# The first RMS norm's reciprocal square roots by one power on GpSimd for each half of the rows

## The chip, the cores and the metric

The kernel runs on one core of a Trainium2 chip. The core has TensorE (matrix products and transposes), VectorE, ScalarE and GpSimd for elementwise work, and SyncE, whose queue issues nearly all transfers. The metric is the time of one execution on the device in microseconds, the median of several runs; less is better.

## The reference

The program computes one layer of a hybrid decoder for 1024 rows of 1024 numbers. It begins with an RMS norm:

```python
def rms_norm(x, g):
    xf = x.astype(jnp.float32)
    y = xf * lax.rsqrt(jnp.mean(xf * xf, axis=-1, keepdims=True) + EPS)
    return (y * g.astype(jnp.float32)).astype(x.dtype)
...
    h = rms_norm(x, norm_mix_g)
    proj = h @ w_in
```

The columns of `proj` feed a gated delta rule, an attention over keys that an indexer selects, and two gates. Their merged result goes through an output product onto `x`; a second norm and a squared-ReLU MLP follow. The change is in the first norm alone: in the 1024 values of `rsqrt(mean + EPS)`, one for each row.

## The kernel before

The 1024 rows are eight blocks of 128, one row to a partition, in two halves of four blocks. `norm1(half)` (L279) prepares a half: ScalarE sums the squares of three blocks and VectorE those of the fourth, which gives `nss`, four columns for a half; VectorE makes `nms`, the mean plus EPS; ten small operations of `rsq_w` (L103) make `nr`, its reciprocal root, from a bit-level first guess and three Newton steps. The blocks are then scaled by `nr` (the first half in the tiles `pj`, by VectorE; the second in tiles that a profile calls `w` and `irl`, shared by VectorE and ScalarE). TensorE transposes them into the PSUM banks `sq`, two groups of 128 columns at a time, and there are two such banks. `ht_out` (L322) takes each group out twice: ScalarE writes `hh`, the rounded value times the norm's gain, and VectorE writes `hl`, what the rounding left over. A bank is free for the next transposes when `hl` has been taken from it.

Around this stand other works of the same microseconds. `turn_raw` transposes the first half's blocks without the norm and multiplies them with the first weights (`sc`, `ikh` and `iq` in a profile), so that TensorE has products before `nr` is known. `weights` splits the weight tiles `wraw` and `iq` into a rounded part (ScalarE) and a rest (VectorE). `dense` multiplies `hh` and `hl` with these parts; it sets most of TensorE's work until the attention begins.

No engine chooses its next instruction on the chip. The works are generators that a planner (`Weave`) interleaves while the program is recorded, by estimated times and priorities; `_Ordered` records every operation (all of them therefore carry L2502), and each engine then runs its own list in that order, waiting on semaphores where an operand is not ready. A later part of the kernel already takes such roots in one GpSimd instruction: `roots` (L1693) for the second norm's `nr` and two places in the delta rule (`rk`, `fo`). They raise to the power in `mhalf` (L127), a column of −0.5 behind the tile `vecs`, by whose name a profile shows it.

Of the kernel before, what the change touches and what calls it, by code (L numbers as in the profile page):

```python
# [15 lines left out]
OP = mybir.AluOpType  # L16
# [4 lines left out]
P = 128  # L21
# [29 lines left out]
def body(tc, a, out, dbg=None):  # L51
# [4 lines left out]
    def pool(name, bufs=1, side=None, space=None):  # L56
        kw = {}
        if space is not None:
            kw["space"] = space
        elif side is not None:  # L60
            kw["side"] = side
        if space is not DRAM:
            kw["reuse_waits"] = "tile"
        es = ExitStack()
        p = es.enter_context(tc.tile_pool(name=name, bufs=bufs, **kw))
        return p, es
# [16 lines left out]
    cst, cst_es = pool("cst", side="left")  # L83
# [16 lines left out]
    V_, A_, G_, PE_, SY_ = (wv.engine(e, n) for e, n in ((V, "V"), (A, "A"), (G, "G"), (PE, "PE"), (SY, "SY")))  # L100


    def rsq_w(pl, dst, src, n, tag, apart=True):  # L103
        t = pl.tile([P, max(n, 4)], F32, name=tag + "t")[:, :n]
        V_.tensor_scalar(dst.bitcast(I32), src.bitcast(I32), -0.5, float(0x5F3759DF), op0=OP.mult, op1=OP.add)
        for _ in range(3):
            if apart:
                yield
            V_.scalar_tensor_tensor(t, dst, -0.5, src, op0=OP.mult, op1=OP.mult)
            if apart:  # L110
                yield
            V_.tensor_tensor(t, t, dst, op=OP.mult)
            if apart:
                yield
            V_.scalar_tensor_tensor(dst, t, 1.5, dst, op0=OP.add, op1=OP.mult)
# [11 lines left out]
    mhalf = vecs[:, NV:]  # L127
# [4 lines left out]
    nss, nms, nr = (cst.tile([P, NB], F32, name=n) for n in ("nss", "nms", "nr"))  # L132
# [146 lines left out]
    def norm1(half):  # L279
        bs = slice(half * 4, half * 4 + 4)  # L280
        for tb in (4, 6, 7, 5) if half else range(4):
            yield ("x", tb)
            if tb == 4:
                yield ("x", 7)
                yield ("w1hi",)
                yield ("hhi", 0, 3)
            if tb in (3, 5):
                junk = ix.tile([P, S], F32, name="ikl")
                V_.tensor_tensor_reduce(out=junk, in0=xs[tb], in1=xs[tb], op0=OP.mult, op1=OP.add, scale=1.0,
                                        scalar=0.0, accum_out=nss[:, tb:tb + 1])  # L290
                continue
            junk = scp.tile([P, S], BF16, name="tkeq")
            A_.activation(junk, xs[tb], AF.Square, accum_out=nss[:, tb:tb + 1])
        yield
        if half:
            yield ("norm", 0)
        V_.tensor_scalar(nms[:, bs], nss[:, bs], 1.0 / D, EPS, op0=OP.mult, op1=OP.add)
        yield from rsq_w(cst, nr[:, bs], nms[:, bs], 4, "n2", apart=False)
        yield
        yield 1.2  # L300
        wv.done("norm", half)
        for c in range(2):
            for tb in range(4 * half, 4 * half + 4):
                xc = xs[tb][:, c * HALF:(c + 1) * HALF]
                if tb % 2 and half:
                    A_.activation(xc, xc, AF.Copy, scale=nr[:, tb:tb + 1])
                else:
                    V_.tensor_scalar(xc, xc, nr[:, tb:tb + 1], None, op0=OP.mult)
            if c == 0:
                t = wv.t  # L310
        wv.t = t
        yield
        for k in range(0, KT, 2):
            if k > 2 or half:
                yield ("ht", half - (k < 4), (k - 3) % KT)
            ps = ps_.tile([P, 2, HALF], F32, name="sq")
            for j in range(2):
                for i in range(4):
                    PE_.transpose(ps[:, j, i * P:(i + 1) * P], xs[4 * half + i][:, (k + j) * P:(k + j + 1) * P], ident)
                wv.add(0, ht_out(half, k + j, ps[:, j, :]))  # L320

    def ht_out(half, k, ps):  # L322
        g = gm[:, k:k + 1]
        if half:
            yield 0.2
        A_.activation(ht_hi[k][half], ps, AF.Copy, scale=g)
        wv.done("hhi", half, k)
        yield
        V_.scalar_tensor_tensor(ht_lo[k][half], ps, g, ht_hi[k][half].bitcast(F32), op0=OP.mult, op1=OP.subtract)
        yield  # L330
        wv.done("ht", half, k)
# [532 lines left out]
    for half in range(2):  # L864
        wv.add(half, norm1(half))
# [1708 lines left out]
```

## Time and profile before

| | us |
|---|---|
| median of 3 runs | 1741.82 |
| lowest and highest run | 1741.39, 1743.05 |
| the profiled execution | 1743.84 |
| its span, first to last instruction | 1742.1 |
| TensorE busy in the span | 1730.6 |
| VectorE, ScalarE, GpSimd busy | 1271.5, 1038.3, 590.1 |
| GpSimd busy from 10 to 50 us | 0.0 |

All times below are counted from the start of the span. The granted clock of TensorE was 0.999 of full speed over the run. A row of a timeline gives start, length, engine, line, operation, the tile written and the tiles read; rows of the same form that follow each other are merged (x4), and brackets tell how long the engine had been idle and what it waited for. In the chain of waits each piece is time that could not be shorter without the piece before it.

### The profile page before, as it was taken

The numbers are of one execution on the slowest core, as the hardware profiler recorded it, in microseconds if no ns is written. First come the engines' busy times: TensorE is split into PE (matmuls) and PEld (weight loads), VectorE is DVE, ScalarE is ACT, GpSimd is POOL, SyncE is SP. The second block draws the span as 40 slices with busy tenths as digits, with TensorE's granted clock in tenths as the row PEclk, the third lists the DMA queues.
The fourth block names the chain that finished last, engine by engine and source line by source line (L and its number), as shares of the span: only waits on it lengthen the run. The fifth ranks groups of instructions, "written<-read, shape, count | busy, mean of one in ns | idle before, by whom it ended". The sixth has DMA issues, their size and how long they took to land.

```text
span 1742.1 us, 27140 instructions
## 1 busy us (share of the span) xinstructions
PE 1730.6 (99%) x9451; PEld 1454.7 (84%) x9451; DVE 1271.5 (73%) x2300; ACT 1038.3 (60%) x2304; POOL 590.1 (34%) x793
## 2 busy tenths in 40 slices
PE   9999999999999999999999999999999999999999
PEld 7987998888888888888888888888888888888887
DVE  6668568767888897896477686768666677958673
ACT  7466647766777656555366676757776754333331
POOL 0005531654563553655014121413322323522230
PEclk9999999999999999999999999999999999999999
DMA  5631246646786778755475222335445459473241
GB/s 169 156 75 61 74 133 135 155 123 135 161 204 137 173 161 188 165 132 127 137 244 159 70 81 73 110 111 204 139 142 164 160 216 332 133 241 117 97 145 49
DMA packets 441643, 252.14 MB, mean 145 GB/s; under 512 B 234089, under 2 KB 385826, under 8 KB 441506
## 3 DMA queue, kind: packets, MB, share of 16 engines
q1 hardware_dynamic: 441490, 250.41, 51.0%
q8 instruction: 74, 1.21, 0.3%
q14 instruction: 63, 0.52, 0.1%
q10 hardware_dynamic: 16, 0.00, 0.0%
HBM read 169.97 MB, written 80.38 MB: 144 GB/s over the span
## 4 chain that ended last, share of the span: by engine, by line
PE 94%; ACT 2%; DMA 1%; DVE 1%; issue 1%; POOL 1%; SPq 1%; POOLq 0%; DVEq 0%; ACTq 0%
PE dd L2502 57%; PE o L2502 16%; PE s L2502 7%; PE pt L2502 6%; PE cc L2502 2%; PE sq L2502 2%; PE tt L2502 2%; PE oo L2502 2%; PE jj L2502 1%; DMA w<-in_x_dram 1%; SPq L2502 1%; DMA kd<-TDk 0%; POOL hl L2502 0%; ACT pr L2502 0%; ACT hh L2502 0%
## 5 line engine op out<-in xcount | busy, mean ns | idle before, releaser
L2502 PE MATMUL dd<-hh,w 128*128 128x512 f32 x1552 | 510.1, 401 | 0.0
L2502 PEld LDWEIGHTS dd<-hh,w 128*128 128x128 f32 x1552 | 286.8, 189 | 51.6
L2502 PE MATMUL dd<-hl,w 128*128 128x512 f32 x776 | 310.3, 400 | 0.0
L2502 ACT ACTIVATE m<-m 128x512 f32<-128x512 f32 (+1 forms) x240 | 140.0, 625 | 74.0 <-PE dd L2502 27.7
L2502 DVE TENSOR_TENSOR m<-m,m 128x512 fp32r<-128x512 f32 (+2 forms) x184 | 141.1, 795 | 42.9 <-ACT m L2502 37.5
L2502 PEld LDWEIGHTS dd<-hl,w 128*128 128x128 f32 x776 | 146.3, 189 | 25.5
L2502 PE MATMUL dd<-hh,m 128*128 128x512 f32 x504 | 167.0, 395 | 0.2 <-DVE w L2502 0.2
L2502 PE MATMUL dd<-w,hh 128*128 128x256 f32 (+1 forms) x704 | 165.3, 325 | 0.0
L2502 PEld LDWEIGHTS dd<-w,hh 128*128 128x128 f32 x704 | 118.1, 191 | 9.4 <-issue 0.2
L2502 POOL TENSOR_TENSOR sx<-sx,stmp 128x60 f32<-128x60 f32 (+24 forms) x248 | 114.2, 461 | 19.4
L2502 PE MATMUL dd<-w,hl 128*128 128x256 f32 (+1 forms) x352 | 114.1, 324 | 0.0
L2502 PEld LDWEIGHTS dd<-hh,m 128*128 128x128 f32 x504 | 93.9, 188 | 18.3 <-issue 0.6
L2502 POOL TENSOR_TENSOR stmp<-sx,um 128x60 f32<-128x60 f32 (+24 forms) x186 | 82.1, 442 | 79.5 <-DMA QT<-ot 21.7
L2502 DVE TENSOR_SCALAR_CACHE_REDUCE tkeq<-sc,cand 128x384 f16<-128x384 f32 (+3 forms) x128 | 103.0, 805 | 1.9 <-POOL sc L2502 0.6
L2502 DVE TENSOR_TENSOR w<-w,w 128x1024 fp32r<-128x1024 f32 (+1 forms) x63 | 72.3, 1147 | 43.7 <-ACT w L2502 29.9
L2502 POOL TENSOR_TENSOR m<-m,m 128x512 f32<-128x512 f32 x48 | 67.0, 1405 | 102.5 <-ACT m L2502 54.8
L2502 ACT ACTIVATE hh<-m 128x1024 fp32r<-128x1024 f32 x44 | 44.9, 1055 | 94.4 <-PE s L2502 40.7
L2502 PE MATMUL dd<-hl,m 128*128 128x512 f32 x252 | 99.4, 395 | 0.0
L2502 ACT ACTIVATE ha<-m 128x1024 fp32r<-128x1024 f32 x44 | 45.2, 1056 | 83.3 <-PE s L2502 30.8
L2502 PE MATMUL o<-hh,m 128*128 128x512 f32 x264 | 84.9, 390 | 0.0
L2502 ACT ACTIVATE tkcm<-sc,cand 128x1024 f16<-128x1024 f32 x64 | 73.0, 1141 | 1.0 <-POOL sc L2502 0.6
L2502 PEld LDWEIGHTS dd<-w,hl 128*128 128x128 f32 x352 | 67.2, 191 | 4.8 <-DVE hl L2502 0.2
(424 smaller groups left out, 4357.5 us busy)
## 6 DMA issues: line engine op xcount, KB each, us to landing
HD<-m SPq DMA_DIRECT2D x112, 256.0 KB, 2.3
m<-HD SPq DMA_DIRECT2D x56, 512.0 KB, 3.9
w<-in_w_in_dram SPq DMA_DIRECT2D x48, 512.0 KB, 4.4
m<-in_w_mlp_up_dram SPq DMA_DIRECT2D x33, 512.0 KB, 5.4
m<-in_w_mlp_down_dram SPq DMA_DIRECT2D x16, 512.0 KB, 5.2
w<-in_x_dram SPq DMA_DIRECT2D x10, 512.0 KB, 4.2
wraw<-in_w_in_dram SPq DMA_DIRECT2D x4, 1024.0 KB
es<-GC SPq DMA_DIRECT2D x8, 512.0 KB, 4.5
```

The costliest lines, as they stand in the source:

```text
L2502: ins = f(*args, **kw)
```

## The change

One line of `norm1` changes. The ten VectorE operations on 128 x 4 numbers become one GpSimd operation on 128 x 4 numbers, for each half:

```diff
         if half:
             yield ("norm", 0)
         V_.tensor_scalar(nms[:, bs], nss[:, bs], 1.0 / D, EPS, op0=OP.mult, op1=OP.add)
-        yield from rsq_w(cst, nr[:, bs], nms[:, bs], 4, "n2", apart=False)
+        G_.tensor_tensor(nr[:, bs], nms[:, bs], mhalf.to_broadcast([P, 4]), op=OP.pow)
         yield
         yield 1.2
         wv.done("norm", half)
```

`rsq_w` stays for one later use. Because the planner makes the order, the built programs show what moved. VectorE, at the second half of the rows, with what each instruction waits for (`w_230` is block 4; `hl_107` to `hl_111` are still rows of the first half; before, then now):

```order
L2502 TENSOR_SCALAR nms<-nss 128x4 [waits DVE_49,Activation_49]
L2502 TENSOR_SCALAR nr<-nms 128x4 [waits DVE_49]
L2502 SCALAR_TENSOR_TENSOR n2t<-nr,nms 128x4 [waits DVE_49]
L2502 TENSOR_TENSOR n2t<-n2t,nr 128x4 [waits DVE_49]
L2502 SCALAR_TENSOR_TENSOR nr<-n2t,nr 128x4 [waits DVE_49]
...
L2502 SCALAR_TENSOR_TENSOR hl_107<-sq,gm,hh_106 128x512 [waits PE_49,Activation_49]
L2502 SCALAR_TENSOR_TENSOR hl_109<-sq,gm,hh_108 128x512
L2502 SCALAR_TENSOR_TENSOR hl_111<-sq,gm,hh_110 128x512 [waits PE_49,Activation_49]
L2502 TENSOR_SCALAR w_230<-w_230,nr 128x512 [waits DMAHW0_49,DVE_49]
```

```order
L2502 TENSOR_SCALAR nms<-nss 128x4 [waits DVE_49,Activation_49]
L2502 SCALAR_TENSOR_TENSOR hl_107<-sq,gm,hh_106 128x512 [waits PE_49,Activation_49]
L2502 SCALAR_TENSOR_TENSOR hl_109<-sq,gm,hh_108 128x512
L2502 SCALAR_TENSOR_TENSOR hl_111<-sq,gm,hh_110 128x512 [waits PE_49,Activation_49]
L2502 TENSOR_SCALAR w_230<-w_230,nr 128x512 [waits DMAHW0_49,Pool_49]
```

The ten operations are gone (of the last three of them, which come three times, one set is shown); `hl` now stands right behind `nms`, and the scaling of block 4 waits for GpSimd. In the first half, likewise, the scaling of `pj` stands right behind `nms` and waits for GpSimd. On GpSimd itself the two powers are inserted behind the memsets of the program's start and ahead of the masks of the indexer's scores:

```order
 L2502 MEMSET iq 128x8x40
 L2502 MEMSET sc_150 128x128
+L2502 TENSOR_TENSOR nr<-nms,vecs 128x4 x2
 L2502 AFFINE_SELECT sc_146<-sc_146 128x128
 L2502 AFFINE_SELECT sc_147<-sc_147 128x128
```

Nothing else moved: but for these rows and the numbers of later buffers, the lists of TensorE, VectorE, ScalarE, GpSimd and SyncE are the same, and on ScalarE only the first scaling of the second half waits for GpSimd in place of VectorE.

## The prediction

> **What bounds the kernel now.** I read the page's engine summary first, then its chain that ended last, then the windows of the first 50 us, since the edited code runs only there, then the chain and the timeline of those microseconds row by row.
>
> ```profile
> span 1742.1 us, 27140 instructions
> PE 1730.6 (99%) x9451; PEld 1454.7 (84%) x9451; DVE 1271.5 (73%) x2300; ACT 1038.3 (60%) x2304; POOL 590.1 (34%) x793
> ...
> PE 94%; ACT 2%; DMA 1%; DVE 1%; issue 1%; POOL 1%; SPq 1%; POOLq 0%; DVEq 0%; ACTq 0%
> ```
>
> TensorE is busy for 99% of the span and carries 94% of the chain: the whole run holds 1742.1 − 1730.6 = 11.5 us in which TensorE does nothing. A change away from TensorE can win only what it takes out of these. The windows tell how many of them lie near the first norm (columns: length, then busy time of PE, PEld, DVE, ACT and POOL, then the granted clock and the DMA share):
>
> ```profile
> 10.00:20.00 10.00, 9.17 (x43) 5.57 (x42) 8.34 (x24) 8.10 (x13) 0.00 (x0) 1.00 0.95 338
> 20.00:30.00 10.00, 8.82 (x64) 7.43 (x62) 8.97 (x24) 9.94 (x18) 0.00 (x0) 1.00 0.50 152
> 30.00:40.00 10.00, 9.33 (x63) 8.30 (x62) 8.62 (x17) 5.96 (x10) 0.00 (x0) 1.00 0.01 2
> 40.00:50.00 10.00, 10.00 (x82) 9.82 (x81) 5.39 (x10) 4.44 (x7) 0.00 (x0) 1.00 0.36 117
> ```
>
> TensorE idles 0.83, 1.18 and 0.67 us in the first three, 2.7 us together, and not at all from 40 us. GpSimd is empty from 10 to 50 us, so nothing is queued ahead of the new powers. Between 20 and 30 us it is ScalarE that has no gap (9.94 of 10.00), and the chain there runs through it:
>
> ```profile
> 25.30 1.31 ACT hh L2502 x3
> ...
> 27.00 0.75 ACT w L2502
> ...
> 27.77 0.74 DVE hl L2502
> ...
> 30.10 0.67 DVE hl L2502
> ...
> 30.91 1.06 PE sq L2502 x8
> ```
>
> None of the twenty instructions that go stands in this chain; VectorE enters it at 27.77, after the last of them.
>
> **The change, first half of the rows.** The timeline of VectorE, ScalarE and TensorE around it (start, length, instruction, idle time before):
>
> ```profile
> 10.94 0.17 DVE L2502 TENSOR_SCALAR nms<-nss 128x4 f32<-128x4 f32 x1
> 11.15 0.17 DVE L2502 TENSOR_SCALAR nr<-nms 128x4 int32<-128x4 int32 x1
> ...
> 13.12 3.26 DVE L2502 TENSOR_SCALAR pj<-pj,nr 128x512 f32<-128x512 f32 x8
> 13.15 4.46 PE L2502 MATMUL dd<-sc,iq 128*128 128x512 f32 x10
> ...
> 17.45 1.91 PE L2502 MATMUL sq<-ident,pj 128*128 128x128 f32 x16
> ...
> 18.52 2.42 ACT L2502 ACTIVATE hh<-sq,gm 128x512 fp32r<-128x512 f32 x4 [1.79 <-PE sq L2502]
> ...
> 19.82 0.75 DVE L2502 SCALAR_TENSOR_TENSOR hl<-sq,gm,hh 128x512 fp32r<-128x512 f32 x1 [1.17 <-ACT hh L2502]
> ```
>
> Removed: ten operations from 11.15 to 13.12, 1.97 us of VectorE. Added: one power of 4 elements per partition. The trace has it with 1, 2 and 8 elements, on the same constant operand (of rk and fo: shortest, median and longest in ns, first and last start; of nr: sum in us, mean in ns):
>
> ```profile
> L2502 POOL TENSOR_TENSOR rk<-ke,vecs x8: 1633/1644/1654, 286.2 to 741.7; 128x8 f32<-128x8 f32 x8
> ...
> L2502 POOL TENSOR_TENSOR nr<-nms,vecs 128x2 f32<-128x2 f32 x3 | 2.1, 710 | 1.8 <-DVE nms L2502 1.8
> L2502 POOL TENSOR_TENSOR nr<-nms,vecs 128x1 f32<-128x1 f32 x2 | 1.1, 560 | 0.1
> ...
> 962.59 0.17 DVE L2502 TENSOR_SCALAR nms<-nss 128x2 f32<-128x2 f32 x1
> ...
> 962.83 0.71 POOL L2502 TENSOR_TENSOR nr<-nms,vecs 128x2 f32<-128x2 f32 x1 [0.24 <-DVE nms L2502]
> ...
> L2502 POOL TENSOR_TENSOR fo<-fe,vecs x8: 1633/2064/3065, 407.7 to 864.7; 128x8 f32<-128x8 f32 x8
> ```
>
> From 2 to 8 elements it grows by (1644 − 710) / 6 = 156 ns each, so four cost 710 + 2 × 156 = 1.02 us. The way there is 962.83 − 962.76 = 0.07 us; the way back I set equal, 0.07. From the end of nms to the first user of nr that is 1.16 us against 13.12 − 11.11 = 2.01, so VectorE scales pj 0.85 us earlier, at 12.27. Bounds of the power: from below the 0.71 of two elements; from above the 3.07 that eight took at worst while VectorE was at work (fo's longest). I take 1.02, since VectorE is idle while it waits here.
>
> What is it worth? TensorE works through the raw products (sc, iq) from 13.15 until the transposes of pj at 17.45, and the four tiles that these read first were scaled by 13.12 + half of 3.26 = 14.75: 2.7 us to spare already. VectorE then falls idle for 1.17 us anyway, until ScalarE's hh, which waited 1.79 us for TensorE's sq. The 0.85 us joins that idle time: **0.0 us**. The cover is 1.17 us, so a path through GpSimd of up to 2.01 + 1.17 = 3.18 us costs nothing either.
>
> **The change, second half of the rows.** Here something moves:
>
> ```profile
> 24.38 0.17 DVE L2502 TENSOR_SCALAR nms<-nss 128x4 f32<-128x4 f32 x1 [0.68 <-ACT tkeq L2502]
> 24.58 0.17 DVE L2502 TENSOR_SCALAR nr<-nms 128x4 int32<-128x4 int32 x1
> 24.73 1.26 ACT L2502 ACTIVATE hh<-sq,gm 128x512 fp32r<-128x512 f32 x2
> 24.73 2.42 ACT L2502 ACTIVATE hh<-sq,gm 128x512 fp32r<-128x512 f32 x4
> ...
> 26.36 0.17 DVE L2502 SCALAR_TENSOR_TENSOR nr<-n2t,nr 128x4 f32<-128x4 f32 x1
> 26.45 2.07 DVE L2502 SCALAR_TENSOR_TENSOR hl<-sq,gm,hh 128x512 fp32r<-128x512 f32 x3
> ...
> 27.00 0.74 ACT L2502 ACTIVATE w<-w,nr 128x512 f32<-128x512 f32 x1
> ...
> 29.46 1.06 ACT L2502 ACTIVATE w<-iq 128x1024 fp32r<-128x1024 f32 x1
> 30.41 1.27 ACT L2502 ACTIVATE hh<-sq,gm 128x512 fp32r<-128x512 f32 x2
> 30.91 0.41 PE L2502 MATMUL sq<-ident,w 128*128 128x128 f32 x2 [0.67 <-DVE hl L2502]
> ...
> 31.71 1.41 DVE L2502 SCALAR_TENSOR_TENSOR hl<-sq,gm,hh 128x512 fp32r<-128x512 f32 x2 [0.95 <-ACT hh L2502]
> 33.36 0.38 PE L2502 MATMUL sq<-ident,w 128*128 128x128 f32 x2
> ```
>
> The power runs from 24.62 to 25.64. VectorE no longer waits for nr before hl; it is free at 24.55. But hl needs hh, and these rows show hl starting when the second hh of a pair ends (30.41 + 1.27 = 31.68, hl at 31.71). Of the four hh from 24.73 to 27.15 the first two end at 25.99, so hl starts at 26.03 in place of 26.45: of 1.90 us freed, **0.42** is used. VectorE keeps this 0.42 through the three hl, the four scalings and the fourth hl, whose end at 30.01 + 0.75 = 30.76 lets TensorE start the next transposes 0.15 later. That start moves from 30.91 to 30.49.
>
> ScalarE gains nothing: its w<-w,nr at 27.00 follows hh without a gap and had its nr, done at 26.53, waiting. Now nr is there at 25.71, with 1.29 us to spare in place of 0.47. So w, the rounding of iq at 29.46 and hh at 30.41 stay where they are, and with them the pair of hl at 31.71, which ends at 33.12. The next transposes need the bank that this pair reads: earliest 33.12 + 0.15 = 33.27. TensorE, 0.42 early, would come at 32.94 and wait; before it came at 33.36. Left of the 0.42: 33.36 − 33.27 = **0.1 us**. From 40 us TensorE has no gap, so I let the 0.1 stand to the end.
>
> **Sum.** 0.0 + 0.1 = 0.1 us less. The profiled execution took 1743.84 us, 1.7 around its span of 1742.1 and 2.0 above the runs' median of 1741.82; against the median I say **1741.7 us**, no change. This kernel's measurement can tell about 0.2% (3.5 us) from no change. The ends of the power's price: at 0.71 the sum stays, as nr is nowhere last; at 3.07 the first half still costs nothing (0.07 + 3.07 + 0.07 = 3.21, against the 3.18 of cover), and in the second nr comes at 27.76, holds ScalarE's w by 0.76 and the pair of hl with it, so that the transposes come at 34.03: 0.7 us more.
>
> **Rivals.** (1) *The ten operations are on the path.* Then both halves' gains count: 0.85 + 1.90 = 2.75 us, 1739.1. For it speaks TensorE's wait of 0.67 us for hl at 30.91; against it that ScalarE is full from 20 to 30 us and that the chain of waits has no n2t. A part of it, that the 0.42 survives whole because the pair of hl at 31.71 is not what holds the bank, gives 1741.4.
>
> (2) *GpSimd starts its first arithmetic late, and the kernel becomes slower.* Before, its first two-operand operation comes at 131.97; now it would be the power at 11 us, with the DMA at 95% in the window. The price decides from 3.18 us in the first half and, in the second, from 1.16 + 1.29 = 2.45 us of path. The rows give little for it:
>
> ```profile
> 131.97 5.05 POOL L2502 TENSOR_TENSOR pj<-pj,qng 128x2048 f32<-128x2048 f32 x1 [2.37 <-DVE pj L2502]
> 169.77 4.60 POOL L2502 TENSOR_TENSOR pj<-pj,qng 128x2048 f32<-128x2048 f32 x1 [7.05 <-DVE cand L2502]
> ```
>
> The first is 0.45 us longer than its twin. Once 0.45 on 1.16 is inside the cover. If every path took 4 us, the second half would cost 4.0 − 2.45 − 0.1 = 1.5 us, 1743.3 (the first half's excess of 0.8 us ends ahead of the same gate and isn't added); to be over 3.5 us slower it needs a path of 6.1 us. The rows side against that: 0.45 us, and the earliest of the eight rk, at 286.2 the program's first power, lies with the rest between 1633 and 1654 ns. The Trainium skill speaks for it (GPSIMD Engine Reference, Instruction dispatch): the first call of a freshly loaded kernel on that engine pays about 6 us, which no instruction shows. By an estimate from that page the first path would be 1.16 + 6 = 7.2 us, hl near 19.8 would come 4.0 us late, and the time would be at most 1745.8.
>
> (3) *The shift changes when transfers of later stages meet.* A tenth of a microsecond has no such lever in the rows, but one of either sign of a few us can't be excluded.
>
> **How the numbers follow.** The forecast with its neighbours from −0.4 to +0.7 us: 0.85. Rival 1 whole: 0.05, still inside 0.2%. Rival 2: 0.05, a fifth of it past 3.5 us. Rival 3: 0.05, evenly either side. Faster by over 0.2% is half of rival 3 and a quarter of rival 1, should more follow from it: 0.04. Slower is the other half of rival 3 and the far fifth of rival 2: 0.04. The rest, 0.92, is no change. The range goes nearly down to rival 1 at 1739.1 and takes in the runs' own scatter (1741.39 to 1743.05) and rival 2 at a path of 4 us: 1739.4 to 1743.9.
>
> **What would show it.** In the changed profile: two powers of about 1.02 us near 11.2 and 24.6; pj scaled from 12.3; VectorE idle longer before hl near 19.8; hl at 26.0; ScalarE's rows from 24.7 to 31.7 unmoved; TensorE's transposes at 30.5 and then at 33.3, with an idle entry before these that was not there. It would be wrong if ScalarE's w<-w,nr waited for GpSimd, if hl after 31 us moved with the rest, or if the spans differ by more than 3 us.

## The result, and the profile after

| | before | after |
|---|---|---|
| median, us | 1742.28 | 1760.42 |
| lowest and highest run | 1741.39, 1743.05 | 1759.26, 1760.56 |
| the profiled execution | 1743.84 | 1760.52 |
| its span | 1742.1 | 1758.8 |

Before has one run more here than in the table ahead of the prediction. The ratio is 1.0101 with a 95% interval of [1.0088, 1.0113]: the kernel became about 18 us slower, where 1741.7 was forecast with a range of 1739.4 to 1743.9. The prediction was wrong, by 16.7 us between the two profiled spans.

The page of the kernel after, its span and its engines:

```profile
span 1758.8 us, 27122 instructions
PE 1747.3 (99%) x9451; PEld 1452.6 (83%) x9451; DVE 1273.0 (72%) x2280; ACT 1038.8 (59%) x2304; POOL 592.3 (34%) x795
```

TensorE is idle for 1758.8 − 1747.3 = 11.5 us, exactly as before. All of the 16.7 us is therefore TensorE *busy* time (1730.6 to 1747.3), with the same 9451 products. No engine waits longer anywhere that counts; the products themselves take longer.

Before following that, the stretch that the prediction spoke of. The timeline of the kernel after, first half of the rows and then second half (start, length, instruction, idle time before):

```profile
10.87 0.17 DVE L2502 TENSOR_SCALAR nms<-nss 128x4 f32<-128x4 f32 x1
11.13 1.02 POOL L2502 TENSOR_TENSOR nr<-nms,vecs 128x4 f32<-128x4 f32 x1 [8.85 <-DVE nms L2502]
...
12.19 3.26 DVE L2502 TENSOR_SCALAR pj<-pj,nr 128x512 f32<-128x512 f32 x8 [1.14 <-POOL nr L2502]
...
15.92 2.36 DVE L2502 TENSOR_TENSOR w<-wraw,w 128x1024 fp32r<-128x1024 f32 x2 [0.48 <-ACT w L2502]
...
19.64 0.75 DVE L2502 SCALAR_TENSOR_TENSOR hl<-sq,gm,hh 128x512 fp32r<-128x512 f32 x1 [1.35 <-ACT hh L2502]
...
24.19 0.17 DVE L2502 TENSOR_SCALAR nms<-nss 128x4 f32<-128x4 f32 x1 [0.68 <-ACT tkeq L2502]
24.44 1.02 POOL L2502 TENSOR_TENSOR nr<-nms,vecs 128x4 f32<-128x4 f32 x1 [12.29 <-DVE nms L2502]
...
25.83 2.07 DVE L2502 SCALAR_TENSOR_TENSOR hl<-sq,gm,hh 128x512 fp32r<-128x512 f32 x3 [1.47 <-ACT hh L2502]
...
26.82 0.74 ACT L2502 ACTIVATE w<-w,nr 128x512 f32<-128x512 f32 x1
...
30.29 0.41 PE L2502 MATMUL sq<-ident,w 128*128 128x128 f32 x2 [0.67 <-DVE hl L2502]
...
33.08 0.41 PE L2502 MATMUL sq<-ident,w 128*128 128x128 f32 x2 [0.21 <-DVE hl L2502]
```

From 24 us this execution runs 0.18 to 0.19 us ahead of the one before (`nms` at 24.19 for 24.38, ScalarE's `w<-w,nr` at 26.82 for 27.00). Read with that offset, each forecast time is met within 0.02 us: the power 1.02 us, `hl` 26.03 − 0.19 = 25.84 (25.83), the transposes 30.49 − 0.19 = 30.30 (30.29) and 33.27 − 0.19 = 33.08 (33.08), the last with the new idle entry of 0.21. The loss is not here.

The windows of TensorE's full stretches show it (columns as in the prediction: length, then busy time and count of PE, PEld, DVE, ACT, POOL, then the granted clock). Before, then after:

```profile
1250.00:1350.00 100.00, 100.00 (x443) 82.80 (x442) 64.87 (x96) 67.57 (x130) 28.92 (x21) 1.00 0.48 155
1500.00:1600.00 100.00, 100.00 (x443) 82.78 (x442) 77.32 (x72) 37.12 (x37) 33.73 (x10) 1.00 0.55 184
```

```profile
1250.00:1350.00 100.00, 100.00 (x433) 81.03 (x432) 63.32 (x92) 68.68 (x134) 29.83 (x22) 1.00 0.45 152
1500.00:1600.00 100.00, 100.00 (x443) 82.81 (x442) 76.75 (x73) 37.60 (x38) 36.03 (x10) 1.00 0.54 184
```

In the same 100 us, at the same clock of 1.00 and without a gap, TensorE does 433 products in place of 443 at 1250 us, and again 443 at 1500 us. So the step from one product to the next grew in one stage and not in the next. The groups of TensorE's products over the whole span (busy time in us, mean of one in ns), before and after:

```profile
L2502 PE MATMUL dd<-hh,w 128*128 128x512 f32 x1552 | 510.1, 401 | 0.0
...
L2502 PE MATMUL dd<-w,hh 128*128 128x256 f32 x448 | 82.6, 285 | 0.0
```

```profile
L2502 PE MATMUL dd<-hh,w 128*128 128x512 f32 x1552 | 515.6, 404 | 0.0
...
L2502 PE MATMUL dd<-w,hh 128*128 128x256 f32 x448 | 80.8, 282 | 1.0 <-DVE w L2502 1.0
```

Products of 512 columns became longer; those of 256 columns became *shorter*. The order of TensorE's records is the same in both traces, so each can be set against its twin. TensorE's start is 0.24 us ahead at 36 us and 0.10 ahead at 139 us, then behind: 0.9 us at 188 us, 4.1 at 384, 8.5 at 873, 11.9 at 1228, 16.7 at 1454, and 16.7 to the end. A loss that grows with the number of products and then stops is no late start and no single wait.

**What had moved.** `rsq_w` allocates a scratch tile, `n2t`, in the pool of constants: 16 bytes on each partition, in a slot of 32. Without the call there is no `n2t`, and every tile that was allocated behind it starts 32 bytes lower: in the built programs 51 tiles by name, among them all of `hh`, `hl`, `ha`, `la`, and the first `m` (m0 to m2 of the last stage). The pools that grow from the other end of the memory (`w0` to `w7`, and the rest of `m`, m3 to m15, m17 and m18) stay. A product has two operands: the stationary one, which an instruction of its own loads ahead of it (PEld in the page), and the moving one, whose columns it then works through. Before, all of these tiles start at the same remainder, so that in each of the 6240 rounded (fp32r) products of 512 columns the two start at addresses that agree modulo 256 bytes. After, 4152 of the 6240 differ by 32 or by 224 (−32), and so do 672 of the 784 of 256 columns. After about 1445 us both operands come from the moved tiles, agree again, and the step is the old one.

Summed over the pairs of twins, by what their operands do after the change: 3301 products of 512 columns with the stationary operand 32 bytes above the moving one, +15.3 us; 441 with it 32 below, +2.0; 657 of 256 columns, −1.9; all the rest, +1.2 (16.7 in all). That accounts for the loss, but as a correlation. The runs had to tell it from the power itself and from its altered rhythm.

### The profile page after: what moved, and what is told of

Same layout as the page of the kernel before. It is cut to its first block, busy times and chain, and to the rows that moved or that the text cites. A ratio compares the mean times of both kernels' runs of the same rounds, so it can differ in the third digit from the quotient of the medians.

```text
span 1758.8 us, 27122 instructions
## 1 busy us (share of the span) xinstructions
PE 1747.3 (99%) x9451; PEld 1452.6 (83%) x9451; DVE 1273.0 (72%) x2280; ACT 1038.8 (59%) x2304; POOL 592.3 (34%) x795
## 4 chain that ended last, share of the span: by engine, by line
PE 95%; DVE 2%; ACT 1%; DMA 1%; SPq 1%; issue 1%; DVEq 0%; ACTq 0%
PE dd L2502 57%; PE o L2502 16%; PE s L2502 7%; PE pt L2502 6%; PE cc L2502 2%; PE sq L2502 2%; PE tt L2502 2%; PE oo L2502 2%; PE jj L2502 1%; SPq L2502 1%; DMA irl<-in_x_dram 1%; DVE pr L2502 0%; DVE hl L2502 0%; DVE cand L2502 0%; ACT hh L2502 0%
## 5 line engine op out<-in xcount | busy, mean ns | idle before, releaser
L2502 PE MATMUL dd<-hh,w 128*128 128x512 f32 x1552 | 515.6, 404 | 0.0
L2502 PEld LDWEIGHTS dd<-w,hh 128*128 128x128 f32 x704 | 116.9, 189 | 11.8 <-DVE w L2502 1.3
L2502 PE MATMUL dd<-w,hl 128*128 128x256 f32 (+1 forms) x352 | 114.0, 324 | 0.0
```

What stands on the lines that cost most here:

```text
L2502: ins = f(*args, **kw)
```

## The experiments

The theory: the loss comes from where the tiles start, and the power costs nothing. The rivals: the power on GpSimd (its operation, or the shifted rhythm behind it) slows TensorE; or the absolute place of the tiles does, not their relation. All kernels compute the whole reference, and in each the instructions of every engine stand in the order of before or of after. Steps given below are mean times from one product's start to the next, up to 1440 us, worked out from the trace's records where the next product has the same form; steps over 250 ns, which hold a wait or an irregular start, are left out. The ratios are worked from all runs of both kernels and need not be the quotients of the two medians.

### The two parts of the change, apart

The changed kernel with the scratch tile allocated and never used:

```diff
+        if half == 0:
+            cst.tile([P, 4], F32, name="n2t")
         G_.tensor_tensor(nr[:, bs], nms[:, bs], mhalf.to_broadcast([P, 4]), op=OP.pow)
```

> The changed kernel, with 32 bytes per partition left unused where the Newton steps' scratch tile n2t stood, so that every tile in SBUF lies where it lay before the change; the instructions and their order are those of the changed kernel. Theory A (the 18 us come from the tiles' places: without n2t the left stack of tiles lies 32 bytes lower, and products whose two operands start at different remainders of 64 bytes step 233 ns in place of 227): the loss is gone, 1741.5 to 1742.5 against 1742.3 before, and the remaining difference is the 0.1 us that the prediction gave to the power itself. Theory B (the power on GpSimd, by its early use or by what it changes in the semaphores, slows what follows): 1760 as before this edit.

The kernel before, all ten operations on VectorE, with the scratch in a tile that exists anyway, so that nothing is allocated for it:

```diff
-        t = pl.tile([P, max(n, 4)], F32, name=tag + "t")[:, :n]
+        t = (pl.tile([P, max(n, 4)], F32, name=tag + "t") if apart else c64(egd))[:, :n]
```

> The kernel before, with its twenty VectorE operations, but their scratch is the tile egd, which is not in use yet, in place of n2t; so the left stack lies 32 bytes lower as in the changed kernel, and no power is on GpSimd in the first norm. Theory A: as slow as the changed kernel, 1759 to 1761, with the 512-column products at 233 ns. Theory B: 1742, as before.

| | median, us | before on the same chip | ratio [95%] | span |
|---|---|---|---|---|
| power, tile kept | 1744.93 | 1743.68 | 1.0004 [0.9995, 1.0013] | 1743.1 |
| ten operations, no tile | 1760.41 | 1743.68 | 1.0095 [1.0078, 1.0112] | 1758.8 |

The window at 1250 us, of the power with the tile kept and of the ten operations without it:

```profile
1250.00:1350.00 100.00, 100.00 (x443) 82.84 (x442) 64.37 (x97) 67.42 (x130) 28.34 (x21) 1.00 0.47 153
```

```profile
1250.00:1350.00 100.00, 100.00 (x433) 81.08 (x432) 62.55 (x92) 68.55 (x134) 30.33 (x22) 1.00 0.46 153
```

443 products with the power, 433 without it: the count follows the tile, not the operation. The second kernel has the very span of the changed one (1758.8) with every VectorE instruction of before. This refutes both forms of the rival with the power, and it measures what the prediction meant to forecast: the power alone is worth no change. (Its median lies above the 1741.5 to 1742.5 that I expected; the kernel before took 1743.68 in the same set.)

The first kernel's trace is 0.7 us ahead of before's until 557 us and ends 1.0 behind. The waits of TensorE, of this kernel and of before, show why:

```profile
PE jj L2504 <- ACT am L2504: 2.2, 1, 2.2
```

```profile
PE jj L2502 <- ACT am L2502: 0.6, 1, 0.6
```

This one wait is 1.6 us longer. It varies between kernels whose instructions are alike (2.1, 1.9, 1.5 and 1.3 us in four of those below), so I put it down to no edit.

### Both stacks moved down

The changed kernel with a 32-byte pad as the first tile at the other end of the memory, so that `w` and the rest of `m` go down by 32 bytes as well. All tiles then stand elsewhere, and agree with each other.

```diff
+    padr, padr_es = pool("padr", side="right")
+    padr.tile([P, 8], F32, name="padr")
```

> The changed kernel, with 32 bytes of unused space at the top of the right stack, so that its tiles move by the same 32 bytes as those of the left stack did: all operands start at a multiple of 64 bytes, none at a remainder of 32. Theory A (only the difference of the two operands' starts counts): back to 1742. Rival C (a start at a multiple of 64 is slow by itself, whatever the other operand does): slower than the changed kernel, as 6240 products in place of 4152 would pay: 1768. Theory B: 1760.

It took 1743.33 against 1743.68, ratio 0.9997 [0.9988, 1.0006]:

```profile
1250.00:1350.00 100.00, 100.00 (x443) 82.83 (x442) 64.39 (x96) 67.40 (x131) 29.77 (x21) 1.00 0.47 153
```

With all of these tiles 32 bytes lower nothing is lost, so it isn't the place by itself; the difference between the two ends counts.

### How far apart

The kernel before, with an unused tile of so many floats behind the constants, which lifts all that follows at its end of the memory by four times as many bytes:

```diff
+    cst.tile([P, 8], F32, name="padc")     # or 16, 32, 64, 128
```

> The kernel before, moved by 32 bytes the other way, up in place of down, with the twenty VectorE operations and n2t as they were. Theory A: the same loss as the changed kernel's, 1759 to 1761, steps near 233 ns. If only the changed kernel's place were bad: 1742.

> The kernel before, with 64 bytes per partition of unused space ahead of the left stack's large tiles. The two operands of 4152 products of 512 columns then differ by 64 modulo 128, and agree modulo 64. Theory A with 64 bytes as the period: no change, 1742. If the period were 128 bytes or more, these products would be slow: 1755 to 1765. Theory B says nothing on it beyond 1742.

> The kernel before, with 128 bytes of unused space ahead of the left stack's large tiles: the two operands of 4152 products differ by 128 modulo 256. Theory A with a period of 128 bytes: no change, all steps of 512 columns at 228. With a period of 256 or more: up to the 5 to 7 us that the shift by 64 cost.

> The kernel before, with 256 bytes of unused space in the same place: 4152 products of 512 columns with operands half of the supposed period apart. By the step that a few of them showed in the run of the 256-column edit, 230.8 against 228.0 ns: 4152 x 2.8 = 12 us more, 1754 to 1757. If 256 bytes were a period: 1743.

> The kernel before, with 512 bytes of unused space ahead of the left stack's large tiles. The shift by 128 cost as much as one by 32, so the period is longer than the 64 or 128 bytes first supposed; over all runs so far the step of 512 columns depends on the operands' difference modulo 512 alone (0: 228.4 ns, 32 or 480: 233, 64: 233.1, 448: 229.8, 128 or 384: 232.4, 256: 230.8). Theory A with a period of 512 bytes: no change, 1.000 of the kernel before, steps at 228. If the period is longer (the tiles are 4096 bytes long): slower by 5 us or more.

| lifted by | median, us | before | ratio [95%] | step of 512 columns, ns (stationary − moving, mod 256) |
|---|---|---|---|---|
| 0 (before) | | | | 228.0 (0) |
| 32 | 1762.91 | 1743.50 | 1.0108 [1.0090, 1.0127] | 233.2 (224), 233.1 (32) |
| 64 | 1750.94 | 1743.68 | 1.0040 [1.0025, 1.0055] | 229.8 (192), 233.1 (64) |
| 128 | 1760.56 | 1743.50 | 1.0095 [1.0081, 1.0109] | 232.3 (128) |
| 256 | 1743.26 | 1743.26 | 0.9997 [0.9987, 1.0007] | 228.0 (0) |
| 512 | 1745.38 | 1743.26 | 1.0009 [1.0000, 1.0019] | 228.0 (0) |
| −32 (after) | 1760.42 | 1742.28 | 1.0101 [1.0088, 1.0113] | 232.9 (32), 232.6 (224) |

The window at 1250 us of the tiles lifted by 128 and by 256 bytes:

```profile
1250.00:1350.00 100.00, 100.00 (x433) 81.26 (x433) 62.61 (x92) 68.29 (x134) 30.52 (x22) 1.00 0.47 154
```

```profile
1250.00:1350.00 100.00, 100.00 (x443) 82.81 (x442) 65.16 (x97) 67.55 (x130) 27.84 (x21) 1.00 0.47 154
```

So 32 bytes up cost about what 32 down cost (1.0108 and 1.0101, with intervals that overlap). At 64 bytes the direction does matter: 233.1 ns with the stationary operand 64 above the moving one, 229.8 with it 64 below. Three of my expectations fell here. I had thought that 64 bytes apart might count as together, or else cost 13 us and more; the kernel took 7.3 us more, because most of its products are of the cheaper direction. I had thought the same of 128 bytes; 232.3 ns says not. Then, from the padded slots below, I expected 256 bytes to cost some 12 us; the step is 228.0 and the ratio 0.9997. The agreement that counts is modulo 256 bytes. Within it the price isn't even: 192 costs 1.8 ns a product, 32, 64, 128 and 224 cost 4.3 to 5.2.

### Only some of the tiles

The kernel before, with 32 bytes put in behind the pool of `hh` and `hl`: these stay with `w`, and only the tiles allocated behind that pool are lifted. Most products then agree.

```diff
+    padm, padm_es = pool("padm", side="left")
+    padm.tile([P, 8], F32, name="padm")
```

> The kernel before, with 32 unused bytes between the tiles hh and hl and the rest of the left stack: hh and hl stay, the tiles above them (those of the attention's keys, and ha, la and m of the last stage) move. Only 600 of the 6240 products of 512 columns then have operands that differ modulo 128. Theory A with the measured steps (228.0 ns where they agree, 232.9 where they differ by 32 or 96): 600 x 4.9 ns = 2.9 us more than before, so 1.0017 of it. If the loss were owed to hh and hl alone: none.

It took 1750.98 against 1743.50, ratio 1.0039 [1.0026, 1.0053], 6.6 us of span where I expected 2.9. The 541 products that now differ, with some 150 that stand beside them, take 3.9 us; the wait for `am` told of above is 1.5 longer; and the 5171 agreeing products are 0.3 ns longer each (1.7 us together), which I can't explain; other steps are about 0.5 us shorter. So the effect goes with the products that differ, as the theory has it, but of the 6.6 us it explains only 3.9.

### Can the gain of the 256-column products be had alone?

Products of 256 columns are *faster* when apart: 119.7 ns together, 116.9 at 224 bytes, 118.3 at 32, 114.0 at 64. Two kernels with the power and the tile kept tried to set only these apart. In the first, all eight weight slots become 128 bytes longer and the units of 256 columns start 64 bytes in:

```diff
-        return w8.tile(shape, dt, name=f"w{i}")
+        t = w8.tile([P, S + 32], dt, name=f"w{i}")[:, off:off + S]
...
+            off = 16 if u else 0
```

> The changed kernel with the 32 bytes kept as in the first experiment, and with the weight tiles of the 256-column products alone begun 64 bytes later in their slots (each slot 128 bytes longer), so that the 672 products of 256 columns differ by 64 modulo 128 and the 4152 of 512 columns agree. The run moved up by 64 showed 114.0 ns a step for such products against 119.7: 672 x 5.7 ns = 3.8 us less work for TensorE, of which waits on the other engines may take a part: 0.998 to 1.000 of the kernel before. If the shorter step is not owed to the operands' places: 1.000.

1753.72 against 1743.50, ratio 1.0056 [1.0042, 1.0070]. The longer slots set every second slot 128 bytes off the rest, and 1443 products of 512 columns ran at 232.5 ns: my misstep, and one more case of the same effect. It also tells which stationary operand counts. Here 320 products agree with their own, but not with the next product's, which is loaded meanwhile: they take 232.1 ns. Another 316 agree with the next one's and not with their own: 233.2. Where both agree it is 228.7, where both are apart 232.3, and the same products take 228 ns in the kernel before. So either one being apart is enough, and both together cost no more. In the second kernel, the four slots of the rounded parts are lengthened by 512 bytes, and the rounded halves of those units start 448 bytes in:

```diff
+        t = w8.tile([P, S + P], dt, name=f"w{i}")[:, off:off + S]
...
-            sp = [(slot(2 * (u % 2) + j, [P, kn, 1024 // kn], F32R), ...
+            sp = [(slot(2 * (u % 2) + j, [P, kn, 1024 // kn], F32R, 112 if u else 0), ...
```

> The changed kernel with the 32 bytes kept, and of the 256-column products' weight tiles only the rounded halves begun 448 bytes into slots that are 512 bytes longer: 448 of these 672 products then have operands 64 apart modulo 512, and all products of 512 columns agree modulo 512. By the steps of 114.4 and 119.5 ns: 448 x 5.1 = 2.3 us less work for TensorE, 0.9985 to 1.000 of the kernel before, if other waits do not take it. The place of the 512-column operands is what the edit with the 64 bytes had spoilt.

1742.37 against 1743.26, ratio 0.9993 [0.9984, 1.0002]. The trace has about half of the gain that I expected, 440 products at 117.3 in place of 119.7 ns, 1.2 us together, but the runs can't tell it from no change. The difference of 64 gave less here than in the kernel lifted by 64 bytes (114.0), where all of these products differ by 64 and not two in three. No version beat the kernel before.

## Why the prediction was wrong

**What held.** Each term of the sum came true. Four elements cost 1.02 us, the interpolated price, both times. The way through GpSimd is 12.19 − 11.04 = 1.15 us in the first half (1.16 forecast). The first half gave 0.0, with one detail off: VectorE's idle time before `hl` near 19.8 grew only to 1.35 in place of 1.17 + 0.85, because the splitting of `wraw` takes a part of it, waiting for ScalarE (0.48 at 15.92). In the second half 0.42 shrank to 0.1 behind the bank that the pair of `hl` reads. The choice of 1.02 us over the 3.07 of `fo` was right, but the rows don't settle its reason (VectorE idle): the `rk` at 530.22 took 1.65 us with VectorE at work throughout. And the upper end of the power's price would have passed the cover of the first half by 0.03 us (3.21 against 3.18), where the prediction says that it costs nothing. With the tile kept, the change is what was forecast: ratio 1.0004 [0.9995, 1.0013].

**What failed.** The step "from 40 us TensorE has no gap, so I let the 0.1 stand to the end", and the sum above it, which has only instructions and waits as terms. A stage without gaps can still change its *step*. I compared the lists of instructions of the built programs, found that nothing else moved, and took that for the whole change; where the tiles start in memory was not compared. The missing term is +16.7 us of span: the price of 4152 + 672 products with operands set 32 bytes apart. Worked from the steps it is 4152 × (232.9 − 228.0) = 20.3 less 672 × (119.7 − 116.9) = 1.9, 18.4 us, against 16.7 by the twins and 18.1 between the medians. (In the later sets the kernel before had medians of 1743.26 to 1743.68; against these the medians too differ by about 17.)

**The rivals.** Rival 1, the ten operations on the path, would have been faster; the power with the tile kept shows no such gain, and the idle entry of 0.21 at 33.08 shows that the bank does hold back the 0.42. Rival 2 had the right sign and the wrong mechanism: the program's first arithmetic on GpSimd began 0.09 us after `nms` ended and took 1.02 us, no longer than the second power. The rule from the Trainium skill (GPSIMD Engine Reference, Instruction dispatch), about 6 us for the first call of a freshly loaded kernel on that engine, does not show for this operation at this place; the trace decides. Rival 3, transfers that meet otherwise, came nearest in that it looked for a small shift with a long lever, but it allowed a few us and named transfers; the waits of TensorE for transfers are not where the time went, as its idle time is 11.5 us on both sides. Of the signs I named, one did fire: spans that differ by more than 3 us.

**The range** of ±2 us came from bounds of the terms in the sum alone, and the chances of 0.92 for no change assumed that these were all the terms there are.

## What to carry to other kernels

An edit that allocates or frees even 16 bytes can move every tile allocated behind it (51 here): compare the tiles' start addresses as well as the instructions, above all where one operand of the products comes from the moved end and the other from the fixed one. When TensorE is busy 99% on both sides and its idle time is equal, look at the step between products (count per 100 us at the same clock), not at waits. To test an edit apart from its allocation, keep an unused tile of the same size in the old place.

## What the runs showed of the hardware

Unexpected was that the step of rounded (fp32r) products depends on where the two operands start relative to each other. With 512 columns it is 228.0 ns in the kernels where all moving and stationary tiles agree modulo 256 bytes, and 229.8 to 233.2 for products whose own do not; with 256 columns it is 119.7 where they agree and 114.0 to 119.4 where they do not. The granted clock is 0.998 to 1.0 in all these runs, and the weight loads take no longer: 188 ns each for `dd<-hh,w` after and 189 before, and 1452.6 us in all against 1454.7.

It is enough that the stationary operand loaded during the product is apart, or that the product's own is (232.1 and 233.2 ns, shown for 128 bytes in the kernel with the padded slots).

Three things stay open: what in the chip does it; why 64 and 192 bytes differ; and why agreeing products that stand among others lose a little too (before 1440 us, those with both stationary operands in agreement take 229.2 ns in the changed kernel and 228.1 as twins before).
